# The second half's input enters the kernel already transposed: its rows are read only for their scales

## The chip, the cores and the metric

The kernel runs on one core of a Trainium2 chip. A core has five engines with a queue of instructions each, served in order: TensorE (PE), VectorE (DVE), ScalarE (ACT), GpSimd (POOL) and SyncE (SP, which here issues all the large DMAs). They meet only through semaphores. The metric is the device time of one execution in microseconds (us), lower is better.

## The reference

One decoder layer over 1024 tokens of 1024 channels, float32. The part that matters here is its beginning: an RMS norm of the input, and one wide projection of the normed input, from which a token mixer takes a recurrent branch (RWKV) and a convolution branch.

```
h = _rms_norm(x, norm_pre_mix)         # x * rsqrt(mean(x*x, channels) + 1e-6) * g
p = h @ w_in                           # 1024 x 2784
u, q = p[..., :1024], p[..., 1024:]
q = q + (_token_shift(q) - q) * mu     # r, k, v, decay, iclr and gate inputs
... recurrence over tokens (r, k, v, w, a, g), 8 heads of 64
c = u[..., :512] * sigmoid(u[..., 512:]); causal depthwise convolution of width 31; layer norm; silu
x = x + _rms_norm(concat(rwkv, c) @ w_out, g2)
x = x + _rms_norm(_conv_ffn(_rms_norm(x, g3)), g4)
```

## The kernel before, in words

**Layout.** Everything is computed channels first: a tile has 128 channels on the partitions and tokens along its free side. The tokens go in two halves of 512, the recurrence in four quarters of 256 with four chunks of 64 each. Float32 products are made from a high and a low part: `split` (L162) casts a tile to its high part on ACT and subtracts that on DVE or POOL for the low one, and `project` (L315 and on, matmuls under L135) adds high*high, high*low and low*high into one PSUM bank, 24 matmuls of 128x512 for a block of 128 output channels. A half's normed input is held in `hs`, eight pairs of tiles `h` from a pool of 16 buffers, so the second half's pairs can only be written when the first half's last projection has read the old ones.

**Projections.** `project(h, hs, names)` in `mixer` runs the blocks named: k0, k1, r0, r1, v0, v1 are two banks each, w and g one, u0 to u3 two each (`glu_in`). Half 0 goes k0 w k1 r0 r1 v0 v1 g u0 u1 u2 u3, and u3 is its last. Weights pass through three raw buffers `wr` (SP), are cast by ACT (`wh`) and, in half 0, subtracted by POOL (`wl`) and stored (`lows`); half 1 reads `wl` back by DMA and needs no POOL for it. The banks `pb` are two; one is free again when `shift` (L344 on ACT, L346 and L350 on DVE) or the gate (L389, L401) has read it.

**Second half's input.** Before the change its eight pieces of four 128-token row tiles are loaded at the start, into buffers that nothing else needs yet (`mixr`, `ck`, `co`). `norm_rows` (L293 to L312) takes the mean square of each row tile, on ACT by Square with an accumulated sum (L308) for even tiles and on DVE by bn_stats (L301) for odd ones, POOL takes the power (L157), and ACT (L311) and DVE (L312) scale the rows in place. When u3 is done, `channels(rows, hs)` turns them: four PE transposes (L150) fill a bank with one tile of 128 channels by 512 tokens, ACT writes the high part with the channel gain (L277), and DVE the low part from the bank and the high part (L279). That is done eight times, over the banks pe, pb, pb.

**Convolution.** `conv(h, i)` makes one 128-channel tile: ACT puts the first tap into the one bank `pc` (L413, waiting for what used that bank before), and 30 DVE steps (L416) add a tap each, the last writing `co`. conv(0,0) may begin when u0 is there; conv(0,1), (0,2), (0,3) follow.

**Recurrence.** Per quarter: `elementwise`, `scores` (L540, L541 on DVE behind PE), `inverses` (L582 transposes, then L591 and L593 in turn, all on DVE), `merge` (L601, L605 on DVE, then PE and ACT), and four chunks (`values`, `recurrence`; L725 is a chunk's last DVE step). `finish(q, j)` norms what two chunks gave and multiplies the gate in (L740 to L760 on DVE). `w_out(0)`, the first output product, reads half 0 of that after splitting it (L162, tiles `m`).

**Order.** Nothing is ordered by hand. Each part is written within a stream with a priority (first, rwkv, top, norm, conv, proj, in this order), and a list scheduler lays all instructions into the five queues when the kernel is built.

Of the kernel before, what the change touches and what calls it, by code (L numbers as in the profile page):

```python
# [22 lines left out]
P = 128  # L23
SEQ = 1024
D = 1024
# [73 lines left out]
class Trunk:  # L99
# [187 lines left out]
    def load_rows(self, h, rows):  # L287
        for t, row in enumerate(rows):
            rs = slice(h * HALF + t * P, h * HALF + (t + 1) * P)
            for j in range(2):  # L290
                self.nc.sync.dma_start(row[j], self.a["x"][rs, j * 512:(j + 1) * 512])

    def norm_rows(self, rows):  # L293

        nc = self.nc
        for t, row in enumerate(rows):
            ss = self.small.tile([P, 4], F32, tag="ss", name=self.nm("ss"))
            if t % 2:
                bs = self.small.tile([P, 4, 6], F32, tag="gn", bufs=3, name=self.nm("bs"))[:, 0:2]
                for j in range(2):  # L300
                    nc.vector.bn_stats(bs[:, j], row[j])  # L301
                nc.vector.bn_aggr(ss[:, 0:2], bs)

                nc.vector.scalar_tensor_tensor(ss[:, 2:3], ss[:, 0:1], ss[:, 0:1], ss[:, 1:2], ALU.mult, ALU.add)
            else:
                for j in range(2):
                    junk = self.tl("pt", [P, 512])
                    nc.scalar.activation(junk, row[j], AF.Square, accum_out=ss[:, j:j + 1])  # L308
                nc.vector.tensor_tensor(ss[:, 2:3], ss[:, 0:1], ss[:, 1:2], ALU.add)
            self.rstd(ss[:, 3:4], ss[:, 2:3], 1.0 if t % 2 else 1.0 / D, RMS_EPS)  # L310
            nc.scalar.activation(row[0], row[0], AF.Copy, scale=ss[:, 3:4])  # L311
            nc.vector.tensor_scalar(row[1], row[1], ss[:, 3:4], None, ALU.mult)  # L312


# [930 lines left out]
    def mixer(self, sts):  # L1245
# [80 lines left out]
        def channels(rows, hs):  # L1326
            with self.stream("norm"):
                self.channels(rows, "pre_mix", hs, slice(0, HALF), ("pe", "pb", "pb"))

# [13 lines left out]
        project(0, hs, "k0 w k1 r0 r1")  # L1343
        with self.stream("norm"):
# [123 lines left out]
```

## Time and profile before

| | us |
|---|---|
| median of 3 runs (1273.63 to 1274.7) | 1274.12 |
| the profiled execution | 1273.13 |
| its span | 1271.4 |
| PE busy | 1220.3 (96%) |
| DVE busy | 891.2 (70%) |
| ACT busy | 731.1 (58%) |
| POOL busy | 495.4 (39%) |

The profiled execution is 1.0 us below the median, and 1.7 us of it lie outside the span. The mixer takes about half of the span: projections of half 0 from 20 to 182 us, of half 1 from 195 to about 390, then w_out(0). A row of a timeline gives start, length, engine, line, operation, output and inputs with buffer numbers left out; a bracket holds the idle time before it and what ended it. Lengths of rows overlap a little, since instructions are pipelined; the distance of two starts is what one costs.

### The profile page before, as it was taken

Reading aid. Unit: us, or ns where it says so; the run is one execution under the profiler, and the core shown is the slowest. Engines: PE = TensorE matmul, PEld = TensorE weight load, DVE = VectorE, ACT = ScalarE, POOL = GpSimd, SP = SyncE. Lnnn points to the kernel's source line nnn. Section 1 sums busy time; section 2 is a strip of 40 time slices with the busy share of each in tenths; the row PEclk is TensorE's granted clock in tenths of the full one; section 3 lists DMA queues with packets and bytes.
Section 4 is the critical chain, followed back from the end, with each engine's and each line's share of the span. In section 5 each row is a group of like instructions: output and inputs, shape, how many; then the busy total and the mean of one; then the engine's idle time right before and its main releaser. Section 6 shows DMA issues by size and latency. Waiting matters only on the chain.

```text
span 1271.4 us, 23025 instructions
## 1 busy us (share of the span) xinstructions
PE 1220.3 (96%) x8460; PEld 990.1 (78%) x8460; DVE 891.2 (70%) x1540; ACT 731.1 (58%) x1518; POOL 495.4 (39%) x438
## 2 busy tenths in 40 slices
PE   6999989999999988999999999999999999999996
PEld 4767767787778877788789878778877888888885
DVE  5286998998679989997631165666356779479667
ACT  7563563655845766566744277776555556545451
POOL 4343320011113332344455369898588860000001
PEclk9999998999999999999999999999999999999999
DMA  7644342343343451232345398888522236336523
GB/s 242 173 133 141 117 134 75 94 134 124 110 135 86 122 183 66 85 84 84 101 132 166 112 336 299 292 305 268 173 65 73 79 127 222 99 98 194 173 76 133
DMA packets 105505, 185.70 MB, mean 146 GB/s; under 512 B 15184, under 2 KB 21712, under 8 KB 105392
## 3 DMA queue, kind: packets, MB, share of 16 engines
q1 hardware_dynamic: 105392, 184.23, 46.2%
q8 instruction: 67, 1.10, 0.4%
q14 instruction: 46, 0.38, 0.1%
HBM read 141.58 MB, written 42.60 MB: 145 GB/s over the span
## 4 chain that ended last, share of the span: by engine, by line
PE 55%; DVE 8%; DMA 3%; POOL 3%; issue 2%; ACT 2%; SPq 0%; POOLq 0%; DVEq 0%; ACTq 0%
PE pb L135 26%; PE pe L135 13%; PE xs L135 11%; PE Y L135 2%; DVE pc L416 2%; PE pc L135 2%; POOL wl L162 1%; DVE nrow L1116 1%; DVE x L1100 1%; POOL b L1056 1%; PE pc L150 1%; DMA pt<-mixd 1%; DMA m<-mixd 1%; PE pe L150 0%; DMA b<-ffn_down 0%
## 5 line engine op out<-in xcount | busy, mean ns | idle before, releaser
L162 POOL TENSOR_TENSOR wl<-wr,wh 128x512 fp32r<-128x512 f32 (+1 forms) x181 | 237.2, 1312 | 247.7 <-ACT wh L162 221.0
L162 ACT CAST wh<-wr 128x512 fp32r<-128x512 f32 (+1 forms) x220 | 135.5, 616 | 170.7 <-issue 43.9
L135 PE MATMUL pb<-h,wh 128*128 128x512 f32 (+3 forms) x720 | 229.5, 398 | 2.5 <-ACT wh L162 1.0
L135 PE MATMUL pb<-f,wh 128*128 128x512 f32 x696 | 219.0, 395 | 2.6 <-ACT wh L162 1.5
L416 DVE SCALAR_TENSOR_TENSOR pc<-c,params,pc 128x512 f32<-128x512 f32 x232 | 174.1, 750 | 8.8 <-ACT pc L413 4.8
L135 PEld LDWEIGHTS pb<-h,wh 128*128 128x128 f32 (+2 forms) x720 | 131.8, 188 | 34.9 <-ACT wh L162 2.6
L135 PEld LDWEIGHTS pb<-f,wh 128*128 128x128 f32 x696 | 130.0, 189 | 31.0 <-ACT wh L162 2.8
L135 PE MATMUL pb<-h,wl 128*128 128x512 f32 (+3 forms) x360 | 146.4, 407 | 2.3 <-POOL wl L162 2.1
L135 PE MATMUL pb<-f,wl 128*128 128x512 f32 x348 | 137.9, 397 | 1.5 <-POOL wl L162 1.5
L157 POOL TENSOR_TENSOR ss<-var,mhalf 128x1 f32<-128x1 f32 x16 | 11.0, 692 | 222.6 <-DVE ss L1097 198.2
L1056 POOL TENSOR_TENSOR b<-b,b 128x512 f32<-128x512 f32 x66 | 86.8, 1317 | 2.8 <-issue 0.9
L135 PE MATMUL pe<-f,wh 128*128 128x512 f32 x272 | 84.2, 391 | 0.1
L135 PEld LDWEIGHTS pb<-h,wl 128*128 128x128 f32 (+2 forms) x360 | 67.7, 188 | 20.7 <-POOL wl L162 4.5
L135 PEld LDWEIGHTS pb<-f,wl 128*128 128x128 f32 x348 | 65.7, 189 | 16.9 <-POOL wl L162 3.1
L135 PE MATMUL xs<-f,wh 128*128 128x512 f32 x200 | 62.0, 391 | 0.4 <-DVE act L953 0.4
L135 PEld LDWEIGHTS pe<-f,wh 128*128 128x128 f32 x272 | 50.9, 188 | 10.6 <-ACT wh L162 0.3
L899 DVE SCALAR_TENSOR_TENSOR pt<-pb,params,pt 128x511 f32<-128x511 f32 (+1 forms) x48 | 35.7, 743 | 30.0 <-ACT ecarry L892 29.5
L162 POOL TENSOR_TENSOR wl<-b,wh 128x512 fp32r<-128x512 f32 x36 | 47.0, 1307 | 21.7 <-ACT wh L162 19.8
L135 PE MATMUL pe<-f,wl 128*128 128x512 f32 x136 | 53.7, 395 | 0.7 <-POOL wl L162 0.7
L706 POOL TENSOR_TENSOR XG<-r,GE 64x256 f32<-64x256 f32 x30 | 20.4, 683 | 86.9 <-DVE r L725 82.0
L178 ACT CAST wh<-wr 128x512 fp32r<-128x512 f32 (+2 forms) x44 | 26.5, 604 | 43.1 <-PE pb L135 31.2
L162 ACT CAST wh<-b 128x512 fp32r<-128x512 f32 x36 | 22.2, 617 | 46.8 <-PE pb L135 18.9
(428 smaller groups left out, 2883.7 us busy)
## 6 DMA issues: line engine op xcount, KB each, us to landing
wr<-ffn_up SPq DMA_DIRECT2D x117, 256.0 KB, 2.8
wr<-w_in SPq DMA_DIRECT2D x80, 256.0 KB, 2.9
b<-ffn_down SPq DMA_DIRECT2D x44, 256.0 KB, 4.4
sums<-b SPq DMA_DIRECT2D x44, 256.0 KB, 4.0
wr<-sums SPq DMA_DIRECT2D x44, 256.0 KB, 2.7
lows<-wl SPq DMA_DIRECT2D x40, 256.0 KB, 3.3
wl<-lows SPq DMA_DIRECT2D x40, 256.0 KB, 2.7
b<-ffn_up SPq DMA_DIRECT2D x40, 256.0 KB, 2.7
```

The lines of the kernel that those rows point to most:

```text
L135: return self.nc.tensor.matmul(out, lhsT, rhs, start=start, stop=stop, skip_group_check=skip)
L150: self.nc.tensor.transpose(out, in_, self.con("ident")[:n, :n])
L157: self.nc.gpsimd.tensor_tensor(out, v[:, :n], self.mhalf[:, :n], ALU.pow)
L162: return self.nc.scalar.copy(hi, src), eng.tensor_tensor(lo, src, hi.bitcast(F32), ALU.subtract)
L178: self.nc.scalar.copy(hi, raw)
L416: nc.vector.scalar_tensor_tensor(out, c[:, j:j + HALF], w(j), acc, ALU.mult, ALU.add)
L706: nc.gpsimd.tensor_tensor(x[64:128], R[64:128, gs], w.GE[64:128, c, gs].unsqueeze(2).broadcast_to([64, 4, CH]), ALU.mult)
L899: nc.vector.scalar_tensor_tensor(acc[:, o:], ps[:, :HALF - o], w(j), acc[:, o:], ALU.mult, ALU.add)
L1056: sub = lambda o, x, y, op=ALU.subtract: self.nc.gpsimd.tensor_tensor(o, x, y, op)
L1100: nc.vector.scalar_tensor_tensor(x, f[c], s[:, 1:2], x, ALU.mult, ALU.add)
L1116: nc.vector.tensor_tensor(out, a, b, op)
```

## The change

Half 1's input is also given transposed by the host (`xt`, 8 tiles of 128 channels by 512 tokens). `norm_cols` is a generator that is advanced behind some projections of half 0: after k1, r0, r1 and v0 it loads one row tile each, into two `c` buffers, takes its scale as before (with ACT's squares written over the row) and writes the scale of 128 tokens into `spread`, 128 equal columns (L327 of the new file). After that, four PE transposes put the scales of all 512 tokens on every partition, in bank pc. Behind v1, g and u1 it loads eight tiles of xt and scales each in place by channel gain and token scale, on DVE (L334 of the new file). After u3, `split` makes the eight pairs `h` from them: ACT casts, DVE subtracts for even tiles and POOL for odd ones. The 32 transposes and the L277 and L279 steps of half 1 are gone.

```diff
+    def norm_cols(self, h, cols):
+        nc = self.nc
+        spread = self.tl("t2", [P, 4, P])
+        for t in range(4):
+            row = [self.tl("c", [P, CONV_W - 1 + HALF])[:, :HALF] for _ in range(2)]
+            self.load_rows(h, [None] * t + [row])
+            s = self.row_scale(t, row, lambda r: r)
+            nc.vector.tensor_scalar(spread[:, t], self.con("ident"), 0.0, s, ALU.mult, ALU.add)
+            yield
+        ps = self.bank("pc")
+        for t in range(4):
+            self.transpose(ps[:, t * P:(t + 1) * P], spread[:, t])
+        for k, col in enumerate(cols):
+            nc.sync.dma_start(col, self.a["xt"][h, k])
+            nc.vector.scalar_tensor_tensor(col, col, self.par("pre_mix", k), ps, ALU.mult, ALU.mult)
+            if k % 2:
+                yield
...
-        project(0, hs, "k0 w k1 r0 r1")
-        with self.stream("norm"):
-            two = self.tl("mixr", [P, 2, D])
-            rows = [cut(two[:, t]) for t in range(2)]
-            rows += [tuple(self.tl(n, [P, 512]) for _ in range(2)) for n in ("ck", "co")]
-            self.load_rows(1, rows)
-            with tc.issue_after(self.mark_hi.ins), tc.issue_after(self.mark_lo.ins):
-                self.norm_rows(rows)
+        two = self.tl("mixr", [P, 4, HALF])
+        cols = [two[:, k] for k in range(4)] + [self.tl(n, [P, HALF]) for n in ("ck", "ck", "co", "co")]
+        norm = self.norm_cols(1, cols)
+        def beside(names):
+            for n in names.split():
+                project(0, hs, n)
+                with self.stream("proj"), tc.issue_after(self.load.ins):
+                    next(norm)
+        project(0, hs, "k0 w")
+        beside("k1 r0 r1")
         weave(quarter(0))
-        project(0, hs, "v0 v1 g")
+        beside("v0 v1 g")
         prepare(0)
-        project(0, hs, "u0 u1")
+        beside("u0 u1")
...
         hs = self.pairs("h")
-        channels(rows, hs)
+        with self.stream("norm"):
+            for k in range(KT):
+                self.split(*hs[k], cols[k], k % 2)
...
+    out["xt"] = np.ascontiguousarray(out["x"].reshape(2, HALF, KT, P).transpose(0, 2, 3, 1))
```

**What it moves.** First, PE between half 0's last projection and half 1's first. Before, the last groups of transposes (pe and pb banks) stand ahead of k0 (bank pb_2698):

```order
L150 MATMUL pe_1992<-const,co_680 128x128
L150 MATMUL pb_1978<-const,mixr_676 128x128 x2
L150 MATMUL pb_1978<-const,ck_678 128x128
L150 MATMUL pb_1978<-const,co_680 128x128
L150 MATMUL pb_1985<-const,mixr_676 128x128 x2
L150 MATMUL pb_1985<-const,ck_678 128x128
L150 MATMUL pb_1985<-const,co_680 128x128
L135 MATMUL pe_2067<-l_225_1195,l_226_1196 128x128
L150 MATMUL pb_1999<-const,mixr_676 128x128 x2
L150 MATMUL pb_1999<-const,ck_678 128x128
L150 MATMUL pb_1999<-const,co_680 128x128
L135 MATMUL pb_2698<-h_1934,wh_2701 128x512
```

Now u3's last matmuls (bank pb_1912) are followed at once by k0's first (bank pb_2680):

```order
L135 MATMUL pb_1912<-h_148,wh_1934 128x512
L135 MATMUL pb_1912<-h_147,wl_1935 128x512
L135 MATMUL pb_1912<-h_149,wh_1934 128x512
L135 MATMUL pb_1912<-h_150,wh_1934 128x512
L135 MATMUL pb_1912<-h_149,wl_1935 128x512
L135 MATMUL pb_2680<-h_1956,wh_2683 128x512
L135 MATMUL pb_2680<-h_1957,wh_2683 128x512
L135 MATMUL pe_1465<-lx,lw 128x256
L135 MATMUL xs_97<-XG_2004,l_213_1145 64x64
```

The recurrence's matmuls (xs, Y) that stood ahead of u3's end now stand behind it.

Second, DVE at the first convolution. Before, the merge's transposes (L605) are followed by two bonus products (L571), a gate and conv(0,0) (bank pc_1701):

```order
L601 STREAM_TRANSPOSE dw<-dw 64x16x32
L605 STREAM_TRANSPOSE l_207_1131<-dw 64x16x32 x2
L571 TENSOR_TENSOR pt_756<-pe_1183,v_825 128x512
L571 TENSOR_TENSOR pt_791<-pe_1186,v_910 128x512
L401 SCALAR_TENSOR_TENSOR c_1573<-c_1573,pb_1575 128x512
L465 TENSOR_SCALAR kk_1197<-pe_1204 128x512
L416 SCALAR_TENSOR_TENSOR pc_1701<-c_1573,params,pc_1701 128x512 x4
```

Now four scalings of xt tiles (L334) stand between, and conv(0,0) (bank pc_1723, lines moved by 23) behind them, in the same bank pc:

```order
L624 STREAM_TRANSPOSE dw<-dw 64x16x32
L628 STREAM_TRANSPOSE l_213_1145<-dw 64x16x32 x2
L594 TENSOR_TENSOR pt_743<-pe_1197,v_812 128x512
L334 SCALAR_TENSOR_TENSOR ck_270<-ck_270,params,pc_996 128x512
L334 SCALAR_TENSOR_TENSOR ck_271<-ck_271,params,pc_996 128x512
L334 SCALAR_TENSOR_TENSOR co_272<-co_272,params,pc_996 128x512
L334 SCALAR_TENSOR_TENSOR co_273<-co_273,params,pc_996 128x512
L594 TENSOR_TENSOR pt_778<-pe_1200,v_911 128x512
L439 SCALAR_TENSOR_TENSOR pc_1723<-c_1587,params,pc_1723 128x512 x2
```

Ahead of these rows the inverses of quarter 0 have also moved: they now begin behind g's shift, before they began ahead of it.

Third, SP and ACT. The four xt loads that L334 waits for stand on SP behind the last weight of u1 (wr_1696):

```order
L170 DMA wr_1696<-w_in 128x512
L183 DMA lows<-wl_1639 128x512
L333 DMA co_272<-xt 128x512
L333 DMA ck_270<-xt 128x512
L333 DMA ck_271<-xt 128x512
L333 DMA co_273<-xt 128x512
L170 DMA wr_1789<-w_in 128x512
```

Before, the next weights follow there directly. On ACT, conv(0,1)'s first tap (L436, bank pc_1756) now stands within the casts of half 1's input (h_1956 and on):

```order
L162 CAST h_1956<-mixr_269 128x512
L162 CAST h_1958<-mixr_269 128x512
L178 CAST wh_2683<-wr_2681 128x512
L162 CAST h_1960<-mixr_269 128x512
L503 ACTIVATE pt_1462<-pe_1465,hw_117 128x256
L727 COPY XG_2004<-xs_97 64x256
L727 COPY XG_2007<-xs_98 64x256
L162 CAST h_1962<-mixr_269 128x512
L436 ACTIVATE pc_1756<-c_1674,params 128x512
L162 CAST h_1964<-ck_270 128x512
L178 CAST wh_2701<-wr_2699 128x512
```

Before, it stood 26 rows ahead of the first L277.

More of the change, by code (lines that the diff above doesn't have):

```diff
@@ L296, in norm_rows @@
         for t, row in enumerate(rows):
[L297 to L312, printed above, removed]
+            s = self.row_scale(t, row, lambda r: self.tl("pt", [P, 512]))
+            nc.scalar.activation(row[0], row[0], AF.Copy, scale=s)
+            nc.vector.tensor_scalar(row[1], row[1], s, None, ALU.mult)
+    def norm_cols(self, h, cols):
+        nc = self.nc
+        spread = self.tl("t2", [P, 4, P])
[13 more added lines that the diff above has]
+                yield
     def project(self, src, m, hs, halves=False, kept=None):
```

19 lines of the change are left out of this document (15 added, 4 removed).

## The prediction

> **What bounds the kernel.** I read the page first, then tables of engine time by stretch, PE's waits and the timelines of PE, DVE and SP around the second half's input.
>
> ```profile
> PE 1220.3 (96%) x8460; PEld 990.1 (78%) x8460; DVE 891.2 (70%) x1540; ACT 731.1 (58%) x1518; POOL 495.4 (39%) x438
> PE 55%; DVE 8%; DMA 3%; POOL 3%; issue 2%; ACT 2%; SPq 0%; POOLq 0%; DVEq 0%; ACTq 0%
> ```
>
> PE is the bound: only what PE does or waits for can move the end. In the mixer the stretches (PE, PEld, DVE, ACT, POOL, then the granted clock) say where PE isn't full:
>
> ```profile
> 20.00:180.00 160.00, 155.37 (x1080) 119.29 (x1081) 110.44 (x199) 89.09 (x171) 62.55 (x63) 0.99 0.49 143
> 180.00:200.00 20.00, 15.30 (x153) 11.65 (x152) 19.80 (x31) 12.96 (x26) 1.87 (x3) 0.83 0.19 60
> 200.00:380.00 180.00, 177.58 (x1704) 138.61 (x1703) 144.41 (x277) 107.83 (x216) 20.63 (x31) 1.00 0.38 117
> 190.00:192.00 2.00, 1.34 (x7) 1.10 (x8) 2.00 (x4) 0.11 (x1) 0.00 (x0) 0.67 0.00 0
> 192.00:194.00 2.00, 1.99 (x8) 1.38 (x7) 2.00 (x4) 1.37 (x3) 0.00 (x0) 0.50 0.00 0
> 194.00:196.00 2.00, 1.48 (x7) 1.30 (x7) 2.00 (x4) 1.25 (x4) 0.00 (x0) 0.50 0.00 0
> PE pe L150 <- DVE h L279: 1.6, 1, 1.6
> PE pb L150 <- DVE h L279: 1.2, 2, 0.7
> PE pe L135 <- ACT l L647: 0.8, 1, 0.8
> ```
>
> 180 to 200 us is the worst place: PE 15.30 of 20, clock down to 0.50, while DVE is full (19.80). The waits there are PE's transposes (L150) on DVE's L279. From 200 to 380 PE idles 2.4 us and DVE 35.6. The changed step is therefore on the path, and behind it DVE has room on average.
>
> **The gap.** PE rows, the fourth and fifth being u3's last matmul and k0's first pair; the last is a stretch with L135 alone:
>
> ```profile
> 163.94 0.39 PE L135 MATMUL pb<-h,wl 128*128 128x512 f32 x1
> 164.62 0.39 PE L135 MATMUL pb<-h,wl 128*128 128x512 f32 x1
> 177.00 0.44 PE L150 MATMUL pb<-const,mixr 128*128 128x128 f32 x2
> 181.88 0.39 PE L135 MATMUL pb<-h,wl 128*128 128x512 f32 x1
> 195.37 1.20 PE L135 MATMUL pb<-h,wh 128*128 128x512 f32 x2
> 197.59 0.39 PE L135 MATMUL pb<-h,wl 128*128 128x512 f32 x1
> 182.27:195.37 13.10, 3.12 (x68) 2.46 (x69) 0.82 0.19 61
> ```
>
> From 182.27 (181.88 + 0.39) to 195.37 are 13.1 us. In them L135 (merge and recurrence, needed in any case) is busy 3.1, so 10.0 are transposes and waits. The first group of four, at 177.00, costs another 0.4. k0's first six matmuls take 197.59 - 195.37 = 2.2 us; at full clock three take 164.62 - 163.94 = 0.68, six 1.4: 0.8 for the slow clock. The order lets PE go from u3 straight into k0. **Gain 11.2 us**, if the new `h` are ready.
>
> **What replaces it.** Durations of its steps:
>
> ```profile
> L279 DVE SCALAR_TENSOR_TENSOR h<-pb,params,h 128x512 fp32r<-128x512 f32 x5 | 3.6, 746 | 0.0
> L162 DVE TENSOR_TENSOR m<-co,m 128x512 fp32r<-128x512 f32 x4 | 2.6, 676 | 0.0
> L162 POOL TENSOR_TENSOR wl<-wr,wh 128x512 fp32r<-128x512 f32 (+1 forms) x181 | 237.2, 1312 | 247.7 <-ACT wh L162 221.0
> L162 ACT CAST wh<-wr 128x512 fp32r<-128x512 f32 (+1 forms) x220 | 135.5, 616 | 170.7 <-issue 43.9
> L308 ACT ACTIVATE pt<-ck 128x512 f32<-128x512 f32 x2 | 1.2, 628 | 0.0
> 72.32 0.73 PE L135 MATMUL pb<-h,wh 128*128 128x512 f32 x2 [0.99 <-ACT wh L162]
> ```
>
> Four spread transposes stay on PE: one group as at 177.00, **+0.4**. Eight ACT casts at 0.62 replace eight L277, 4 DVE subtracts at 0.68 and 4 on POOL at 1.31 replace eight L279 at 0.75. A tile is free for them once u3's second-last use of it is past: the two matmuls with `h` of a k end 0.68 us after those of the k before, so casts (0.62) keep step, and k0 reads k = 7 only 4.8 us (7 x 0.68) after its start; POOL has no `wl` in half 1. No PE time.
>
> Earlier, ACT's four squares (0.63 each) and two bn_stats pairs on DVE move from before 30 us, where I give nothing for the room they leave, to beside half 0's projections. One pair of squares stands around a weight cast at the place of the row at 72.32, where PE already waited 0.99 for ACT. One square ahead of a cast there is +0.6, both and a stall's slow clock 1.6; I take **+0.8** (0 to 1.6). Row loads come in pairs behind weights on SP with 2.9 us to landing and no user near: nothing; if that cover fails, the same 0.8 pays for it. The last spread waits for POOL's power behind a `wl` subtract (1.3), DVE with it; DVE is idle for 50 of the 160 us from 20 to 180, so nothing.
>
> **DVE falls behind at conv(0,0).** This is the term I trust least:
>
> ```profile
> 115.93 2.21 DVE L582 STREAM_TRANSPOSE dw<-l 64x512 f32<-64x512 f32 x2
> 120.52 0.73 DVE L350 SCALAR_TENSOR_TENSOR gd<-pb,params,gd 96x511 f32<-96x511 f32 x1
> 132.11 1.29 DVE L571 TENSOR_TENSOR pt<-pe,v 128x512 f32<-128x512 f32 x2
> 135.03 1.55 DVE L416 SCALAR_TENSOR_TENSOR pc<-c,params,pc 128x512 f32<-128x512 f32 x2 [0.32 <-ACT pc L413]
> 171.73 0.75 DVE L416 SCALAR_TENSOR_TENSOR co<-c,params,pc 128x512 f32<-128x512 f32 x1
> 135.59 0.33 SPq L170 DMA_DIRECT2D wr<-w_in  x1
> 137.12 0.38 SPq L170 DMA_DIRECT2D wr<-w_in  x1
> wr<-w_in SPq DMA_DIRECT2D x80, 256.0 KB, 2.9
> L413 ACT ACTIVATE pc<-c,params 128x512 f32<-128x512 f32 x6 | 4.7, 780 | 3.2 <-DVE co L416 3.2
> ```
>
> L582 now stands behind g's shift (120.52 + 0.7 = 121.2 instead of 115.9): 5.3 later, less 1.1 for g's rows that it no longer encloses, plus 0.7 for a gate moved ahead: the merge's transposes end at 137.0 instead of 132.1, the next product at 137.6. Then DVE needs xt. The row at 135.59 is u1's last weight; the four loads follow it on SP at about 137 to 138.5 (0.4 each), and with 2.9 us each, four at once, land at about 142. So L334 ends near 142.7, L413's 0.8 follows, conv(0,0) starts near 143.5 and not 135.0, and with its 37.4 us (135.03 to 172.48) ends at 181. u3 ends on PE at 182.3, less about 2 for recurrence matmuls now behind it, plus 0.8: also 181. L413 of conv(0,1), ahead of five of the eight casts, waits until just then: the cast of k = 4 is done at 182.4, and PE reads it after 4 x 0.68 at 183.7 or later. Just in time.
>
> Next, the banks. DVE's order has 43 us of steps from conv(0,0)'s end to the shift of k1's second bank (28 convolution steps of 0.75, four shifts, four chunk steps, scores). With 0.8 for L413 that is at 225, and r0 needs this bank, the sixth block of half 1. Before:
>
> ```profile
> 232.79 0.74 DVE L350 SCALAR_TENSOR_TENSOR row<-pb,params,row 128x511 f32<-128x511 f32 x1
> 241.66 0.62 PE L135 MATMUL pb<-h,wh 128*128 128x512 f32 x2
> ```
>
> There DVE was 8 us ahead of PE (r0 starts at 241.66, 46.3 after k0). Now PE needs 27.2 for five blocks (24 x 0.227), and of the 18.3 that were beside them (46.3 - 0.8 - 27.2) about four fifths by the number of matmuls, 14.5: it is there at 181 + 41.7 = 222.7. **+2.3** of waiting; 0 if xt lands as DVE asks for it, up to 8 if the small matmuls cost half of that.
>
> **At w_out(0).**
>
> ```profile
> 387.70 0.67 DVE L760 TENSOR_TENSOR mixr<-mixr,pe 128x512 f32<-128x512 f32 x1
> 388.43 0.93 PE L150 MATMUL pe<-const,l 128*128 128x128 f32 x4 [2.19 <-DVE mixr L760]
> ```
>
> PE waits 2.19 for the last `finish`, on which w_out(0) hangs. By summed DVE steps it now stands 2.7 later, behind g's shift instead of ahead of it. I take half, **+1.3** (0 to 2.7): part goes into DVE's 35.6 us of idle time. From there to the first FFN blocks the orders of PE are alike, so what is left stays.
>
> Sum: -11.2 + 0.4 + 0.8 + 2.3 + 1.3 = -6.4. From the profiled execution's 1273.1 that is 1266.7; the median was 1.0 above it: **1267.7**.
>
> **Rivals.** (1) *DVE sets the pace.* The two DVE terms are at their upper ends: 8 + 2.7 instead of 3.6, so -11.2 + 0.4 + 0.8 + 10.7 = +0.7, 1274.8. For it: DVE full from 120 to 200, now with xt to wait for. Against: 35.6 us of DVE idling after 200. (2) *DVE and POOL block each other* at the splits:
>
> ```profile
> 160.67 1.71 DVE L509 TENSOR_TENSOR pt<-pt,row 128x512 f32<-128x512 f32 x1
> 86.11 1.82 POOL L162 TENSOR_TENSOR wl<-wr,wh 128x512 fp32r<-128x512 f32 x1 [1.16 <-ACT wh L162]
> ```
>
> An elementwise step with two inputs in SBUF takes 1.71 here, against 0.68 for the same form of L162; POOL's takes 1.82 against 1.31. Half 1's DVE subtracts have two such inputs, L279 had one input in PSUM, and four POOL subtracts run beside them: 4 x 1.03 = 4.1 more for DVE, and k0 waits for it: 1271.8. Against it: only 4 subtracts, and POOL has little else. The Trainium skill, page SBUF — State Buffer, section "Who interferes with whom", states this as a rule: a DVE instruction with two SBUF inputs and a GpSimd one that reads SBUF exclude each other for the whole instruction. The two rows agree with it; by the page every subtract that meets one pays, which is this rival's time, where my sum lets them miss each other. (3) *All of the gap is won*, the later terms hidden: 1274.1 - 11.2 + 0.4 = 1263.3. (4) *Slower: xt comes late.* L334 heads DVE's queue; the loads stand on SP behind a weight that waits for a free buffer. Whatever they are later than 142, conv(0,0) ends later, L413 holds the casts and PE stands, one for one, from about 1.3 us on. My 6.4 gain is gone at 7.7 us, and 10.2 give 1276.6: xt at 152. For it: DVE's place right behind; against it: the trace has that weight at 135.59 and the next at 137.12, so it needs a wait not seen there. (5) *A step doesn't go away*: the order shows it gone, 0.
>
> **Chances.** 0.2% (2.5 us) is about what a measurement can tell from no change. Forecast 0.45 (1264 to 1271), (3) 0.13, (2) 0.13, (1) 0.15, (4) 0.14. (2) lies on the edge at 1271.6: about half counts as faster. Faster 0.45 + 0.13 + 0.07 and a little of (1)'s lower side, 0.67; same 0.18; slower 0.15. The range reaches from a little under (3) to a little over (1): 1262 to 1275.5, which leaves out most of (4).
>
> **What would show it.** Right: no L150 between u3 and k0, k0 starting near 181 with a granted clock of 1.00 between 186 and 200, conv(0,0) starting at 141 to 144. Wrong: PE idle in front of r0 beyond 5 us or before w_out(0) beyond 4 (1); subtracts of 1.7 us (2); DVE idle in front of L334 beyond 5 us (4).

## The result, and the profile after

| | before | after |
|---|---|---|
| median, same comparison (range) | 1273.88 (1273.49 to 1274.7) | 1287.33 (1285.36 to 1291.98) |
| ratio, 95% interval | | 1.011 (1.0081 to 1.0139) |
| the profiled execution, its span | 1273.13, 1271.4 | 1286.23, 1284.4 |

The change makes the kernel 1.1% slower, about 13.4 us; 1267.7 was forecast. In the changed kernel lines stand 23 further down from `project` on: the chunk's last step L725 is L748, `finish`'s last step L760 is L783. The busy time of the changed kernel from its page, and then the table by stretch (stretch, length, busy time and number of PE, PEld, DVE, ACT, POOL, granted clock, share and GB/s of the DMAs):

```profile
PE 1222.1 (95%) x8432; PEld 987.5 (77%) x8432; DVE 889.5 (69%) x1544; ACT 734.5 (57%) x1518; POOL 502.2 (39%) x442
```

```profile
20.00:180.00 160.00, 151.24 (x1009) 115.05 (x1008) 108.90 (x196) 84.68 (x160) 63.31 (x63) 0.99 0.54 164
180.00:200.00 20.00, 18.89 (x173) 14.56 (x175) 19.52 (x30) 15.42 (x34) 7.79 (x9) 1.00 0.51 158
200.00:380.00 180.00, 178.50 (x1752) 137.95 (x1748) 143.16 (x274) 110.16 (x221) 19.99 (x29) 1.00 0.37 112
380.00:400.00 20.00, 8.69 (x36) 7.15 (x36) 19.89 (x42) 9.06 (x18) 3.36 (x4) 0.57 0.06 13
```

The same stretch of the kernel before, which the prediction did not look at:

```profile
380.00:400.00 20.00, 17.81 (x115) 15.70 (x114) 20.00 (x42) 11.41 (x22) 5.56 (x4) 0.91 0.20 62
```

PE has the same work. The hole at 180 to 200 is closed (15.30 to 18.89 busy, clock 0.83 to 1.00), and a larger one has opened at 380 to 400 (17.81 to 8.69, clock 0.91 to 0.57). DVE is full there in both kernels.

**The gap went as forecast.** PE's timeline: u3's last matmul with `wl`, then k0's first pair with the new `h`:

```profile
182.45 0.39 PE L135 MATMUL pb<-h,wl 128*128 128x512 f32 x1
182.68 0.61 PE L135 MATMUL pb<-h,wh 128*128 128x512 f32 x2
```

k0 starts at 182.68 instead of 195.37, and half 1's projections run 10 to 18 us ahead of before up to 360 us; at their end it is 5.7.

**What hangs on quarter 0 became late.** DVE's timeline of the changed kernel: the row scales (L300, L327), the second `kk` product (L488), g's shift and the inverses' transposes (L373, L605), two of the last xt scalings (L334), conv(0,0) (L439), the first of the two last steps of chunks 0 and 4 (L748; a chunk has two, one for four heads each), the last step of `finish`(1,1) (L783):

```profile
58.34 0.69 DVE L300 BATCH_NORM_STATS2 bs<-c 128x6 f32<-128x512 f32 x1 [2.68 <-DMA c<-x]
59.92 0.69 DVE L300 BATCH_NORM_STATS2 bs<-c 128x6 f32<-128x512 f32 x1 [0.89 <-DMA c<-x]
61.97 1.31 DVE L327 TENSOR_SCALAR t<-const,ss 128x128 f32<-128x128 f32 x1 [0.67 <-POOL ss L157]
63.20 0.68 DVE L488 TENSOR_SCALAR kk<-pe 128x512 f32<-128x512 f32 x1
...
124.00 0.74 DVE L373 SCALAR_TENSOR_TENSOR gd<-pb,params,gd 96x511 f32<-96x511 f32 x1
124.77 2.23 DVE L605 STREAM_TRANSPOSE dw<-l 64x512 f32<-64x512 f32 x2
142.28 1.40 DVE L334 SCALAR_TENSOR_TENSOR ck<-ck,params,pc 128x512 f32<-128x512 f32 x2
145.84 1.54 DVE L439 SCALAR_TENSOR_TENSOR pc<-c,params,pc 128x512 f32<-128x512 f32 x2 [0.25 <-ACT pc L436]
191.03 0.43 DVE L748 TENSOR_TENSOR r<-xs,XG 64x256 f32<-64x256 f32 x1
291.81 0.43 DVE L748 TENSOR_TENSOR r<-xs,XG 64x256 f32<-64x256 f32 x1
395.61 0.67 DVE L783 TENSOR_TENSOR mixr<-mixr,pe 128x512 f32<-128x512 f32 x1
```

The same `kk` product and the same two chunk steps in the kernel before:

```profile
58.36 0.69 DVE L465 TENSOR_SCALAR kk<-pe 128x512 f32<-128x512 f32 x1 [4.43 <-PE pe L135]
179.48 0.43 DVE L725 TENSOR_TENSOR r<-xs,XG 64x256 f32<-64x256 f32 x1
281.42 0.77 DVE L725 TENSOR_TENSOR r<-xs,XG 64x256 f32<-64x256 f32 x2
```

The second `kk` product, on which quarter 0's scores hang, stands behind row scales that wait for their rows (2.68 and 0.89) and for POOL's power (0.67), and is 4.8 us late. The inverses begin 8.8 later (115.93 to 124.77; what adds the other 4 isn't isolated), conv(0,0) 10.8 (135.03 to 145.84), the last steps of chunk 0 11.6 later, those of chunk 4 10.4, of `finish`(1,1) 7.9. This isn't one lateness passed on: chunks 1 to 3 are only 2.6 to 5.5 late, so most of it is won back, and from chunk 4 on they are 9 to 12 late again. From 200 to 380 PE idles 1.5 us, so what makes these chunks late is what stands ahead of them in PE's queue, not a wait of PE. PE pays where w_out(0) needs `finish`(1,1). PE's timeline and its longest wait in the whole kernel:

```profile
390.47 1.09 PE L150 MATMUL pe<-const,mixr 128*128 128x128 f32 x4 [10.37 <-DVE mixr L769]
PE pe L150 <- DVE mixr L769: 11.4, 2, 10.4
```

PE has run out of half 1's projections ahead of that point, stands 10.37 us at `finish`'s transposes, and starts w_out(0) 8.1 us later than before (389.87 to 397.96). The first FFN block is 7.2 late. A second loss comes at the mixer's other end, DVE's rows for the norm of the last convolution tile (L432, now L455) and for the first step behind the second output product (L782, now L805), before and then after:

```profile
621.28 0.80 DVE L432 TENSOR_SCALAR t<-pc,mv 128x512 f32<-128x512 f32 x1
678.36 0.69 DVE L782 TENSOR_TENSOR t<-pb,po 128x512 f32<-128x512 f32 x1 [4.61 <-PE pb L135]
```

```profile
639.98 0.81 DVE L455 TENSOR_SCALAR t<-pc,mv 128x512 f32<-128x512 f32 x1 [0.67 <-POOL mv L157]
690.15 0.69 DVE L805 TENSOR_TENSOR t<-pb,po 128x512 f32<-128x512 f32 x1 [5.35 <-PE pb L135]
```

The last convolution tile is 18.7 late there, and the lateness behind it 11.8 instead of 7.2; at the end of the profiled executions it is 13.1.

### The profile page after: what moved, and what is told of

Its sections match the earlier page's. It is cut to its first block, busy times and chain, and to the rows that moved or that the text cites. A ratio compares the mean times of both kernels' runs of the same rounds, so it can differ in the third digit from the quotient of the medians.

```text
span 1284.4 us, 22981 instructions
## 1 busy us (share of the span) xinstructions
PE 1222.1 (95%) x8432; PEld 987.5 (77%) x8432; DVE 889.5 (69%) x1544; ACT 734.5 (57%) x1518; POOL 502.2 (39%) x442
## 4 chain that ended last, share of the span: by engine, by line
PE 67%; DVE 14%; ACT 5%; issue 4%; POOL 4%; DMA 4%; SPq 0%; POOLq 0%; DVEq 0%; ACTq 0%
PE pb L135 35%; PE pe L135 14%; PE xs L135 12%; DVE pc L439 4%; POOL wl L162 2%; PE Y L135 2%; PE pc L135 2%; POOL b L1079 1%; DVE nrow L1139 1%; PE pe L150 1%; DVE x L1123 1%; DVE sub L614 1%; PE pc L150 1%; DVE dw L616 1%; DMA pt<-mixd 1%
## 5 line engine op out<-in xcount | busy, mean ns | idle before, releaser
L135 PE MATMUL pb<-h,wh 128*128 128x512 f32 (+3 forms) x720 | 230.0, 398 | 4.0 <-ACT wh L162 3.4
L135 PE MATMUL pb<-f,wh 128*128 128x512 f32 x696 | 221.1, 398 | 2.2 <-ACT wh L162 1.1
L439 DVE SCALAR_TENSOR_TENSOR pc<-c,params,pc 128x512 f32<-128x512 f32 x232 | 174.3, 751 | 5.2 <-ACT pc L436 1.4
L135 PEld LDWEIGHTS pb<-h,wh 128*128 128x128 f32 (+2 forms) x720 | 130.7, 187 | 36.8 <-ACT wh L162 5.4
L135 PEld LDWEIGHTS pb<-f,wh 128*128 128x128 f32 x696 | 130.6, 190 | 30.9 <-ACT wh L162 2.5
L135 PE MATMUL pb<-h,wl 128*128 128x512 f32 (+3 forms) x360 | 145.4, 404 | 3.3 <-POOL wl L162 2.1
L135 PE MATMUL pb<-f,wl 128*128 128x512 f32 x348 | 138.7, 399 | 2.1 <-POOL wl L162 2.1
L157 POOL TENSOR_TENSOR ss<-var,mhalf 128x1 f32<-128x1 f32 x16 | 11.2, 704 | 231.5 <-DVE ss L1120 198.8
L135 PE MATMUL pe<-f,wh 128*128 128x512 f32 x272 | 84.2, 391 | 0.1
L135 PEld LDWEIGHTS pb<-h,wl 128*128 128x128 f32 (+2 forms) x360 | 67.4, 187 | 21.7 <-POOL wl L162 4.3
L135 PEld LDWEIGHTS pb<-f,wl 128*128 128x128 f32 x348 | 66.1, 190 | 18.4 <-POOL wl L162 4.6
L135 PE MATMUL xs<-f,wh 128*128 128x512 f32 x200 | 62.0, 391 | 0.4 <-DVE act L976 0.4
L135 PEld LDWEIGHTS pe<-f,wh 128*128 128x128 f32 x272 | 50.8, 188 | 10.6 <-ACT wh L162 0.3
L135 PE MATMUL pe<-f,wl 128*128 128x512 f32 x136 | 53.6, 394 | 1.3 <-POOL wl L162 1.3
L922 DVE SCALAR_TENSOR_TENSOR acc<-pb,params,acc 128x511 f32<-128x511 f32 (+1 forms) x30 | 22.4, 747 | 36.9 <-ACT acc L919 30.4
```

Source lines behind the costliest of these rows:

```text
L135: return self.nc.tensor.matmul(out, lhsT, rhs, start=start, stop=stop, skip_group_check=skip)
L157: self.nc.gpsimd.tensor_tensor(out, v[:, :n], self.mhalf[:, :n], ALU.pow)
L439: nc.vector.scalar_tensor_tensor(out, c[:, j:j + HALF], w(j), acc, ALU.mult, ALU.add)
L922: nc.vector.scalar_tensor_tensor(acc[:, o:], ps[:, :HALF - o], w(j), acc[:, o:], ALU.mult, ALU.add)
```

## The experiments

Ratios are to the kernel before in the same comparison, whose median was 1273.3 to 1274.4. An order is called *dealt* where the scheduler lays it anew, and *kept* where a table holds the instructions that both kernels have in the order of the kernel before.

| run | median, us | ratio | 95% |
|---|---|---|---|
| e1 gap only, dealt | 1286.94 | 1.0100 | 1.0077 to 1.0123 |
| e2 rows early, dealt | 1283.86 | 1.0073 | 1.0054 to 1.0091 |
| e3 no rows, dealt | 1281.88 | 1.0054 | 1.0031 to 1.0077 |
| e4 subtracts on POOL, dealt | 1291.83 | 1.0138 | 1.0112 to 1.0165 |
| e5 before, w_out(0) freed, dealt | 1284.36 | 1.0081 | 1.0053 to 1.0108 |
| e6 after, w_out(0) freed, dealt | 1291.98 | 1.0145 | 1.0122 to 1.0168 |
| e7 before, half the convolution, dealt | 1287.04 | 1.0121 | 1.0088 to 1.0154 |
| e8 after, half the convolution, dealt | 1293.64 | 1.0164 | 1.0138 to 1.0191 |
| e9 gap only, kept | 1273.76 | 0.9997 | 0.9984 to 1.0010 |
| e10 the change in an early form, kept | 1273.20 | 0.9995 | 0.9977 to 1.0012 |
| e11 the change as made, kept | 1290.35 | 1.0131 | 1.0114 to 1.0149 |
| e12 early form, dealt | 1288.57 | 1.0120 | 1.0099 to 1.0140 |
| e13 early form, kept on DVE alone | 1288.29 | 1.0121 | 1.0100 to 1.0141 |

### First four: which part costs?

**e1** is the kernel before, with the transposes replaced by plain splits of its row tiles, which leaves the transposition out of the computation; the gap is taken away and nothing is added.

```diff
-        channels(rows, hs)
+        with self.stream("norm"):
+            for k in range(KT):
+                self.split(*hs[k], rows[k // 2][k % 2], k % 2)
```

> The kernel before with one thing taken out: the second half's transposes. Its h is split straight from the scaled rows (rows taken for channels, without the factors of the channels), so the transposition is left out of the computation; the rows are loaded and scaled where they were, and there is no xt. Theory 1 (early rows): the gap at 180 to 200 us is worth its 10 to 11 us, and the changed kernel lost them because its row work holds up the first quarter; this kernel has no such work, so 1263 to 1265. Theory 2 (slack): the gap lay beside the recurrence, which ends last in front of w_out(0) whatever PE does before; PE then stands about 10 us in front of w_out(0) instead, and the time is 1271 to 1275.

Measured 1.0100: taking work and waits away made the kernel slower, as much as the whole change. Its table by stretch:

```profile
180.00:200.00 20.00, 16.43 (x206) 12.10 (x201) 19.62 (x27) 12.13 (x26) 7.50 (x7) 1.00 0.38 107
400.00:500.00 100.00, 90.83 (x1178) 80.39 (x1178) 79.83 (x149) 61.41 (x149) 28.60 (x30) 0.88 0.41 132
```

Nothing of the row work is in it, so the row work can't be all of the loss. k0 starts at 181.35, 14 us earlier than before, but w_out(0) as before (389.9); from 400 to 500 DVE does 79.8 of 100 us where the kernel before has 91.8, and the first FFN block is 7.6 late, the last chunk 11.0.

**e2** is the change with its rows early, beside the first half's own, and xt beside the same projections as in the change.

```diff
-        project(0, hs, "k0 w")
-        beside("k1 r0 r1")
+        project(0, hs, "k0 w k1 r0 r1")
+        with self.stream("norm"), tc.issue_after(self.mark_hi.ins), tc.issue_after(self.mark_lo.ins):
+            for _ in range(4):
+                next(norm)
...
-        beside("v0 v1 g")
+        project(0, hs, "v0")
+        beside("v1 g")
```

> The changed kernel with the row part (loads, squares, bn_stats, spread) moved back to where the rows were scaled before, behind the first half's channels; the xt tiles are loaded and scaled beside v1, g, u0 and u1. Theory 1 (early rows): elementwise(0), the scores and the merge of the first quarter are back at their old times (second kk product at 58 to 59 us, L605 at 116 to 118), the gap stays won: 1263 to 1266. Theory 2 (slack): the first quarter is back at its old times as well, but what is won at 180 to 200 us is waited for at w_out(0): 1271 to 1275. Rival (DVE falls behind at conv(0,0) because of xt): no better than 1282.

Measured 1.0073. w_out(0) is on time again (389.7), and yet the first FFN block is 6.9 late. xt came late here, as rival (4) had it, on DVE's timeline:

```profile
143.48 0.75 DVE L334 SCALAR_TENSOR_TENSOR co<-co,params,pc 128x512 f32<-128x512 f32 x1 [4.32 <-DMA co<-xt]
```

**e3** is the change without the row part; its output lacks half 1's row scales.

```diff
-        spread = self.tl("t2", [P, 4, P])
...
-            row = [self.tl("c", [P, CONV_W - 1 + HALF])[:, :HALF] for _ in range(2)]
-            self.load_rows(h, [None] * t + [row])
-            s = self.row_scale(t, row, lambda r: r)
-            nc.vector.tensor_scalar(spread[:, t], self.con("ident"), 0.0, s, ALU.mult, ALU.add)
...
-            self.transpose(ps[:, t * P:(t + 1) * P], spread[:, t])
+            self.transpose(ps[:, t * P:(t + 1) * P], self.con("ident"))
```

> The changed kernel without the second half's row part: no row loads, squares, bn_stats and spread; the spread transposes read the identity, so the second half is not scaled by its rows' norms. It prices the row part as a whole. Theory 1: 1262 to 1265. Theory 2: 1270 to 1274. If the loss came from the xt tiles and their scaling on DVE (L334), it is still there: 1283 or more.

Measured 1.0054. w_out(0) starts at 385.96, 12 us earlier than in the change and 3.9 earlier than before; the first FFN block is 5.6 late all the same. So the row part, with the order that is dealt for it, explains what is late at w_out(0) (chunk 4 stands behind 806 projection matmuls on PE in the change, behind 746 in e2 and e3), and something behind it, common to e1, e2 and e3, costs on its own.

**e4** gives all eight subtracts of the splits to POOL, so DVE has less to do and can't meet POOL there.

```diff
-                self.split(*hs[k], cols[k], k % 2)
+                self.split(*hs[k], cols[k], True)
```

> The changed kernel with all eight subtractions of the second half's splits on POOL instead of four on DVE (2.7 us less on DVE between 179 and 188 us). Theory 1 (early rows): no difference to the changed kernel beyond 3 us, 1283 to 1288, since the first quarter is as late as before. Rival (DVE is the bound from 145 to 200 us, and the recurrence is late because DVE is): 2.7 us or more faster than the changed kernel, 1280 to 1284.

Measured 1.0138, no faster than the change (1.011): in the order dealt for it, sparing DVE four steps and the meeting with POOL wins nothing.

### Next four: does DVE's work or w_out(0)'s wait set the end?

**e5** and **e6** let w_out(0) read tiles that are ready early (the convolution's, twice), in the kernel before and in the change; the first half's output product is then of other data.

```diff
-                self.split(*acts[k], mixr[:, k] if k < 4 else co[k - 4])
+                self.split(*acts[k], co[k % 4] if h == 0 else mixr[:, k] if k < 4 else co[k - 4])
```

> The kernel before, with w_out(0) taking the convolution's channels twice: the recurrence's result is left out of the first half's output projection, so w_out(0) no longer waits for the recurrence. Only the wait of 2.2 us in front of w_out(0) can go here: 1270 to 1274 by every theory. It is the other half of the comparison with the next kernel.

> The changed kernel with w_out(0) taking the convolution's channels twice (the recurrence's result left out of it), so that the 10.4 us and the slow clock in front of w_out(0) can't be. Theory 2 (the gap was slack beside the recurrence, and PE now stands where it meets it): w_out(0) starts 5 us earlier than before's, and the time is that of the kernel before with the same edit or up to 5 us less: 1266 to 1273. Theory 3 (DVE's queue or the recurrence sets the pace of the mixer to its end, wherever PE waits): the loss shows up again behind w_out(0), in front of the first FFN block, and the time stays 8 to 13 us above that kernel: 1280 to 1286.

Measured 1.0081 and 1.0145. Nothing is gained in either. In e6 PE still waits 8.0 us, since `finish`(1,1) has transposes of its own ahead of most of w_out(0): the first FFN block starts at 512.9, 8.0 later than in the change. So these two don't tell what the wait alone is worth; they show that an edit of one operand moves the kernel before by 10 us.

**e7** and **e8** leave out every second tap of the convolution, in both kernels (15 of 30 DVE steps in each of eight tiles).

```diff
-        for j in range(1, CONV_W):
+        for j in range(2, CONV_W, 2):
```

> The kernel before with every second tap of the convolution left out (taps 2, 4, ... 30 of 30): 120 steps of 0.75 us, some 90 us, less on DVE in the mixer. Theory 3 (DVE's queue sets the mixer's pace): 15 us or more faster, under 1260. Theory 2 (the latency of the recurrence and PE set it): 1268 to 1273.

> The changed kernel with every second tap of the convolution left out. Theory 3: with room on DVE the recurrence isn't late, and the gap's gain of 5 to 11 us comes through against the kernel before with the same edit. Theory 2: still 5 to 13 us slower than that kernel.

Measured 1.0121 and 1.0164. With DVE relieved of some 90 us (120 steps at 0.75) neither is faster than the same kernel with all of it (1.0121 against 1, 1.0164 against 1.011). In e7 the last `finish` of half 1 is done 15 us earlier, and yet the first FFN block starts 19 us later. In these orders DVE's amount of work doesn't set the end; what less of it would be worth with the order held still was not tried. What e1 to e8 share is that each was laid out anew.

### Last five: the order held still

In **e9** to **e11** a table pins the order of all instructions that both kernels have, by dependences that only order the queue of one engine; new instructions go where the scheduler puts them. **e9** is e1 with the eight subtracts on POOL and before's order on all engines.

```diff
-        channels(rows, hs)
+        with self.stream("norm"), self.free():
+            for k in range(KT):
+                self.split(*hs[k], rows[k // 2][k % 2], True)
...
-        Trunk(ctx, tc, a).run()
+        trunk = Trunk(ctx, tc, a)
+        trunk.run()
+        trunk.pin()
```

> The kernel before without the second half's transposes, like the first experiment (h split straight from the scaled rows, so the transposition is left out), but every other instruction stands on its engine in exactly the order of the kernel before: the order is written into the kernel as a table and held by order-only dependencies. The eight casts and eight POOL subtractions alone are placed freely. Theory 4 (the loss of the first eight experiments is the price of an order dealt anew: each edit made the scheduler set the recurrence's steps elsewhere among the projections and convolution steps): with the order kept, the gap is won and stays won, 1262 to 1267. Theory 2 (slack): PE waits for the recurrence at its next steps instead, and w_out(0) starts no earlier: 1270 to 1275.

Measured 0.9997 (0.9984 to 1.0010). Without the transposes, and with nothing in their place but casts and POOL's subtracts, the kernel takes the time of before: in this order the gap was worth nothing. k0 starts 4.6 us earlier (190.81), w_out(0) 3.3, the first FFN block 0.2 later. Where the 11 us went is best seen in a run that makes the whole change:

**e10** does what the change does with before's order kept (PE, DVE, ACT, SP), in an early form: the rows directly behind the first half's, two of the four in the `mixr` tile, xt beside w, k1, r0 and r1, subtracts on POOL.

```diff
+            row = ([self.tl("c", [P, CONV_W - 1 + HALF])[:, :HALF] for _ in range(2)] if t < 2 else
+                   [cols[2 * t - 4 + j] for j in range(2)])
...
+        project(0, hs, "k0")
+        with self.stream("norm"), tc.issue_after(self.mark_hi.ins), tc.issue_after(self.mark_lo.ins):
+            with self.free():
+                for _ in range(4):
+                    next(norm)
+        beside("w k1 r0 r1")
```

> The changed kernel in its best form, with the order of the kernel before kept on PE, DVE, ACT and SP for all that both have: rows loaded right away into tiles of their own (four c tiles, the mixr tile) and reduced where they were before, xt loaded and scaled beside w, k1, r0 and r1, all subtractions of the splits on POOL. Theory 4: 1262 to 1267, a kernel faster than both. Theory 2 (slack): 1270 to 1275. If the early steps cost as in the second experiment (3 us at 30 us): 3 us more on either.

Measured 0.9995 (0.9977 to 1.0012): the whole change at no cost, and at no gain. PE's timeline at the place of the gap (lines are 80 further down; L215 is L135), and its table by stretch:

```profile
183.86 0.21 PE L215 MATMUL pe<-l 32*32 32x32 f32 x1 [2.12 <-ACT l L751]
187.45 1.06 PE L215 MATMUL pe<-l,dw 32*32 32x32 f32 x16 [1.87 <-ACT dw L769]
189.87 1.22 PE L215 MATMUL pb<-h,wh 128*128 128x512 f32 x2
```

```profile
180.00:200.00 20.00, 15.69 (x177) 12.22 (x177) 19.51 (x25) 11.80 (x26) 11.93 (x10) 0.83 0.25 76
188.00:192.00 4.00, 3.77 (x19) 2.90 (x17) 3.96 (x5) 2.50 (x7) 3.23 (x5) 0.50 0.02 4
```

With no transpose left, PE waits 2.12 and 1.87 for ACT in the merge and recurrence steps that stand there in the order kept: in the kernel before, the transposes stand among these steps. PE is as idle from 180 to 200 as before (15.69 busy against 15.30), and k0 starts 5.5 us earlier, not 11. Of the 4.3 us that are left of it at w_out(0), 0.7 are left at the first FFN block. PE's first row of each, in the kernel before:

```profile
389.87 0.56 PE L135 MATMUL pb<-wh,m 128*128 128x256 f32 x1
497.65 0.70 PE L135 MATMUL pb<-f,wh 128*128 128x512 f32 x2 [0.60 <-DVE f L279]
```

and in e10, with a wait for POOL's low weights between them:

```profile
385.59 0.36 PE L215 MATMUL pb<-wh,m 128*128 128x256 f32 x1
396.32 0.39 PE L215 MATMUL pb<-wl,m 128*128 128x256 f32 x1 [2.15 <-POOL wl L242]
496.91 0.70 PE L215 MATMUL pb<-f,wh 128*128 128x512 f32 x2 [0.62 <-DVE f L359]
```

The kernel before has no wait at that place of w_out(0); e9 has one of 2.15 too.

**e11** is the change as made, with before's order kept (PE, DVE, ACT, SP).

```diff
-                with self.stream("proj"), tc.issue_after(self.load.ins):
+                with self.stream("proj"), tc.issue_after(self.load.ins), self.free():
                     next(norm)
...
+        trunk.pin()
```

> The changed kernel as it was made (rows beside k1, r0, r1 and v0, xt beside v1, g, u0 and u1, splits half on DVE), with the order of the kernel before kept on PE, DVE, ACT and SP for all that both have; the row part, xt scalings and splits are placed among it by the scheduler. Theory 1 (early rows: the row work beside the first quarter holds it up by 4 to 9 us) and theory 4 together: 1268 to 1274, between the kept order's best and before. Theory 1 alone (order without a price): as the changed kernel, 1284 to 1288. Theory 2 (slack): 1275 to 1280.

Measured 1.0131. DVE's timeline at the last xt scalings, SP's row of the loads they wait for, and chunk 4:

```profile
145.67 0.75 DVE L414 SCALAR_TENSOR_TENSOR co<-co,params,pc 128x512 f32<-128x512 f32 x1 [4.66 <-DMA co<-xt]
147.31 0.75 DVE L414 SCALAR_TENSOR_TENSOR co<-co,params,pc 128x512 f32<-128x512 f32 x1 [0.90 <-DMA co<-xt]
142.85 0.92 SPq L413 DMA_DIRECT2D co<-xt  x2
293.64 0.77 DVE L828 TENSOR_TENSOR r<-xs,XG 64x256 f32<-64x256 f32 x2
```

Scores(0) are 4.9 late by the rows, 5.6 more are waits for xt, whose loads stand on SP behind a weight; chunk 0 is 14.2 late, chunks 4 to 7 and `finish`(1,1) 12.2, w_out(0) 11.7, the FFN 12.9. With the order held still, a lateness put into quarter 0 goes through the recurrence to the output product, with 2.5 of 14.2 us won back. Common work stands in the same order in e10 and e11 on PE, DVE, ACT and SP. They differ in where rows and xt stand, in the buffers of the rows, and in the engine of four subtracts, and that is 17.2 us (1290.35 - 1273.20).

**e12** is e10 without the table, and with half of the subtracts on DVE. **e13** is e10 with the table for DVE alone.

```diff
-                self.split(*hs[k], cols[k], True)
+                self.split(*hs[k], cols[k], k % 2)
...
-        trunk.pin()
```

> The changed kernel in the early form of the tenth experiment (rows at once into tiles of their own, xt beside w, k1, r0 and r1), but with the order that the scheduler itself deals for it, and the splits' subtractions half on DVE again. PE's order for it is that of the first experiment. If the order dealt anew is what the first experiment paid for: 1284 to 1289, against 1273 with the order kept. If it isn't: 1271 to 1276.

> The early form of the tenth experiment with the order of the kernel before kept on DVE alone; PE, ACT and SP stand as the scheduler deals them (the recurrence's steps stand behind 13 to 34 more projection matmuls on PE, from the third on). If DVE's order (convolution steps ahead of the recurrence's) is what the dealt order loses by: 1272 to 1277. If it is PE's (projections ahead of the recurrence's steps): 1282 to 1290, with the recurrence's chunks 4 to 7 some 5 us later than in the tenth experiment.

Measured 1.0120 and 1.0121. The same work but for the engine of four subtracts, the same places of its rows and loads: 1273.2 with before's order, 1288.6 dealt anew; for the gap alone (e9 and e1) 1273.8 and 1286.9. Part of the difference can be read in the order of PE, as the number of projection matmuls of half 1 and half 0 that stand ahead of each chunk:

```
chunk    0    1    2    3    4    5    6    7
before 504  552  620  674  734  806  862  914
after  540  590  662  732  806  865  932  986
e1,e12 504  568  620  684  768  817  878  938
e13    504  565  645  696  758  825  888  936
```

A matmul of a projection takes 0.227 us, so 72 of them (chunks 4 and 7 in the change) are 16 us of other work that PE does first, more than the 12.7 us that it is ahead at k0. With DVE's order kept and PE's, ACT's and SP's dealt (e13), chunks 4 and 7 stand 24 and 22 matmuls further back, 5.4 and 5.0 us, and are 5.1 and 6.9 later than before, 8.8 and 10.6 later than in e10. How late (+) or early (-) steps begin, against the kernel before, in us; a chunk goes by the first of its two last steps on DVE, and the last column but one is the first FFN matmul:

| | chunk 0 | chunk 1 | chunk 3 | chunk 4 | chunk 7 | w_out(0) | chunk 10 | FFN | chunk 14 |
|---|---|---|---|---|---|---|---|---|---|
| before, at | 179.5 | 210.9 | 258.2 | 281.4 | 350.7 | 389.9 | 474.7 | 497.7 | 589.1 |
| after | +11.6 | +2.6 | +4.2 | +10.4 | +9.4 | +8.1 | +7.7 | +7.2 | +6.0 |
| e9 gap, kept | +0.7 | -0.1 | -2.8 | -2.8 | -2.7 | -3.3 | +0.2 | +0.2 | -1.4 |
| e10 early, kept | -0.3 | -1.0 | -3.7 | -3.7 | -3.7 | -4.3 | -0.9 | -0.7 | -0.8 |
| e11 as made, kept | +14.2 | +14.9 | +12.2 | +12.2 | +12.3 | +11.7 | +13.3 | +12.9 | +11.4 |
| e1 gap, dealt | -1.0 | -9.9 | -6.9 | -0.8 | -0.8 | 0.0 | +16.5 | +7.6 | +11.0 |
| e12 early, dealt | 0.0 | -8.0 | -4.0 | +2.3 | +2.1 | +3.4 | +19.4 | +10.8 | +14.2 |
| e13 DVE's order alone | +0.3 | -1.0 | +0.4 | +5.1 | +6.9 | +5.7 | +13.9 | +14.6 | +13.4 |

So there are two losses, each as large as the whole: the place of the row and xt work (e11 against e10), and an order dealt anew (e1 against e9, e12 against e10). They don't add: the change has both and loses 13.4. Why not stays open, but the table shows that they don't act at one place. With the order kept (e11) the lateness of chunk 0 stays to the end; in the change it is mostly gone at chunk 1. In the change, e1, e12 and e13, 4.7 to 6.3 us are lost between chunks 3 and 4, where the kept orders lose none. That the order dealt anew costs is shown; that PE's part of it does it, and not ACT's or SP's, is read from e13 and the tables above, and no run kept PE's alone. What makes chunks 8 to 10 late in e1 and e12, behind a w_out(0) that is on time, stays open, as does the last convolution tile's 18.7 in the change.

## Why the prediction was wrong

**"The changed step is therefore on the path"** is the step that failed, and with it the gain of 11.2. That PE idled 180 to 200 us was read as time on the path because PE is the bound of the whole. With the order kept the gain is 0 within 2 us (e9: 0.9984 to 1.0010): 4.6 us of it reach k0, 3.3 w_out(0) and none the first FFN block. Where k0 does start 13 to 14 us earlier (the change, e1, e12, e13), in orders dealt anew, w_out(0) starts 0 to 8.1 us later than before. No run closes the whole gap and keeps all of the rest in order, so the 11.2 us were not tried by themselves. The 13.1 us from 182.27 to 195.37 held 10.0 of transposes and waits, but also a ping-pong between PE and ACT that needs its own time: e10's k0 came 5.5 earlier, not 11.

**"From there to the first FFN blocks the orders of PE are alike, so what is left stays."** It doesn't: in e10 4.3 us at w_out(0) become 0.7 at the first FFN block. Of the 3.5 us that e9 and e10 each give back, 2.15 are the wait for POOL's low weights within w_out(0), shown above for e10; the rest was not isolated.

**The order of the rest.** The sum priced the steps that the order shows moved around the gap, and counted the recurrence's delay on PE as work beside it: "less about 2 for recurrence matmuls now behind it". It did not price where the eight chunks stand among half 1's matmuls, 36 to 72 matmuls further back. No term stood for that.

**"Row loads come ... no user near: nothing", and "+0.8" for the squares.** The user was the second `kk` product, behind the row scales in DVE's queue: 4.8 late. Of PE's early waits, one of 1.61 replaces the 0.99 shown, one of 1.28 and one of 1.23 are new, 3.1 against a term of 0 to 1.6; with quarter 0's lateness and the order dealt for it the part is worth 12 us at w_out(0) (e3 against the change). PE's three rows:

```profile
48.39 0.33 PE L150 MATMUL pc<-const,t 128*128 128x128 f32 x1 [1.23 <-DVE t L327]
67.91 0.73 PE L135 MATMUL pb<-h,wh 128*128 128x512 f32 x2 [1.28 <-ACT wh L162]
76.58 0.73 PE L135 MATMUL pb<-h,wh 128*128 128x512 f32 x2 [1.61 <-ACT wh L162]
```

"DVE is idle for 50 of the 160 us from 20 to 180, so nothing" was wrong in kind: the idle time of a stretch covers nothing for a step whose successor is the next in a chain.

**DVE at conv(0,0), +2.3.** The inverses began at 124.77 instead of the 121.2 worked out, conv(0,0) at 145.84 instead of 143.5, and u3 ended at 182.7 instead of 181. The mark set for conv(0,0), 141 to 144, was missed. PE doesn't wait for DVE in front of r0: the term is 0, inside its range.

**w_out(0), +1.3 (0 to 2.7).** The wait grew by 8.2 (10.37 against 2.19). It was worked out from the DVE steps moved ahead of `finish`, and not from the time at which those steps can begin. DVE's last scores of quarter 2 and the reduction of `finish`(1,1) that stands behind them in its queue, before and then after:

```profile
370.34 0.42 DVE L540 TENSOR_TENSOR l<-pe,const 128x256 f32<-128x256 f32 x1
373.46 0.68 DVE L744 TENSOR_REDUCE gn<-pe 128x8 f32<-128x512 f32 x1
```

```profile
379.49 0.41 DVE L563 TENSOR_TENSOR l<-pe,const 128x256 f32<-128x256 f32 x1
383.53 0.68 DVE L767 TENSOR_REDUCE gn<-pe 128x8 f32<-128x512 f32 x1
```

In both kernels chunk 7's last step on DVE is 23 us past when that reduction comes, and DVE doesn't idle in front of it: `finish` waits there for its turn, not for the chunk. The scores come 9 us later because PE makes them later: the last of them stand behind 1070 projection matmuls, 1010 before.

**The rivals.** The mark set for (1), PE idle before w_out(0) beyond 4 us, was met, its mechanism at most in part: DVE idles 37 of the 180 us from 200 to 380, but is full from 376 us to `finish`'s last step (from 366 in the kernel before). With half of the convolution gone w_out(0) still starts 4.1 us late (e8, in an order of its own). (2) was seen and is small. DVE's four subtracts, and POOL's beside the first, the third and the fourth:

```profile
179.27 1.58 DVE L162 TENSOR_TENSOR h<-mixr,h 128x512 fp32r<-128x512 f32 x1
182.22 0.68 DVE L162 TENSOR_TENSOR h<-mixr,h 128x512 fp32r<-128x512 f32 x1
183.82 0.94 DVE L162 TENSOR_TENSOR h<-ck,h 128x512 fp32r<-128x512 f32 x1
187.39 0.69 DVE L162 TENSOR_TENSOR h<-co,h 128x512 fp32r<-128x512 f32 x1
```

```profile
179.03 1.27 POOL L162 TENSOR_TENSOR h<-mixr,h 128x512 fp32r<-128x512 f32 x1
182.93 1.28 POOL L162 TENSOR_TENSOR h<-mixr,h 128x512 fp32r<-128x512 f32 x1
187.84 1.39 POOL L162 TENSOR_TENSOR h<-co,h 128x512 fp32r<-128x512 f32 x1 [0.30 <-ACT h L162]
```

DVE's first and third, which begin while POOL is at one, take 0.90 and 0.26 longer than the second, 1.2 in all against the 4.1 of this rival; the fourth, which began ahead of POOL's, pays nothing. The Trainium skill, page SBUF — State Buffer, section "Who interferes with whom", states that such a pair excludes each other for the whole instruction; the trace agrees, since both end 0.55 us behind POOL's end (180.85 against 180.30, 184.76 against 184.21), nearly a whole subtract of 0.68. (4) did not occur in the change, where DVE finds xt there at 142.28, but does in e2 (4.32) and in e11 (4.66 and 0.90). Right were the marks for the gap: no L150 between u3 and k0, k0 near 181, clock 1.00. These were met and the time still went the other way: they watched the hole, not what w_out(0) hangs on.

No version beat the kernel before; e10 has its time.

## What to carry to other kernels

Idle time of the busiest engine is worth something only if no other chain ends later: follow the chain that the next large wait hangs on (here w_out(0), `finish`, the scores ahead of it in DVE's queue, and their place in PE's) and ask whether the step delays *that*, before a hole in PE is counted as gain. Where a scheduler lays out the queues, any edit, even one that takes work away, deals the order anew, and that alone was worth 13 to 15 us here; compare the places of the long chain's steps in the whole order, not just around the edit, and try the edit once with the old order kept. New work goes where no step of the chain stands behind it in a queue: with the order kept, the same rows and loads cost 17 us beside quarter 0 and nothing ahead of it.

## What the runs showed of the hardware

The granted clock fell behind some of PE's idle stretches and was back within some us: 0.57 over the 20 us that hold the wait of 10.37 in the change, and in e10 0.50 from 188 to 192 behind two waits of 2, although PE is busy 3.77 of these 4 us, and 1.00 from 196 on. It doesn't fall behind all of them: e1's PE idles 3.6 of the 20 us from 180 to 200 with the clock at 1.00 throughout, and what decides is not shown. So a small wait of PE can cost more than its length, which the prediction had priced at 0.8 for the gap; that in e10 it comes without a loss at the end fits a stretch that isn't on the path.
